# The opening of a conformer block's first FFN, loaded and scheduled in another order

## The chip, the cores and the metric

One kernel launch runs on one core of a Trainium2 chip. The metric is the device time of that launch in microseconds (us). TensorE (PE) multiplies, VectorE (DVE) and ScalarE (ACT) do the elementwise work, GpSimd (POOL) a few small operations, and SyncE (SP) issues the transfers from the chip's memory. Each engine takes its own instructions in the order in which the built program lists them; engines wait for each other through semaphores.

## The reference, cut to what matters

The block works on 256 tokens with 2048 channels, all in float32:

```
ada = silu(c) @ w_ada + b_ada                      # 9 vectors of 2048: shift, scale, gate, three times
h = rms_norm(x, ffn1_norm) * (1 + sc1) + sh1
x = x + 0.5 * g1 * (silu(h @ Wg) * (h @ Wu)) @ Wdown    # FFN 1, 5632 wide
h = rms_norm(x, mix_norm) * (1 + scm) + shm
x = x + gm * mixer(h)                              # differential attention and a causal convolution
h = rms_norm(x, ffn2_norm) * (1 + sc2) + sh2
x = x + 0.5 * g2 * (silu(h @ Wg2) * (h @ Wu2)) @ Wdown2 # FFN 2
```

The change concerns FFN 1, and within it mostly the stretch before and just after the first product with a weight. What must be there before that product: silu(c), the first 128 scale and the first 128 shift values of the modulation (each a dot product of c with a row of `w_ada`), the sums of squares of all 256 tokens, and the first weight tile.

## The kernel before, in words

Every weight is read once, as a tile of 128 x 2048 floats (1 MB): four row tiles of 128 input channels by 512 output columns. A product with a weight is made of three passes (L232, L233, L234): both operands are split into a rounded high part and the exact remainder, and the kernel adds high x high, high x low, low x high. So each weight row tile goes through ACT, which rounds it (`whi`, L222), and through DVE, which subtracts (`wlo`, L224). A row tile takes six passes, three for each of two token tiles. Weights land in four buffers (`raw`), which the adaLN rows share: 144 tiles of `w_ada` (L151) are each multiplied with c and summed in one DVE instruction (L152), two of them (a scale and a shift) for each 128 channels.

FFN 1 is cut into 22 chunks of 256 gate and 256 up columns (here c0 to c21). Stage A takes the first row tiles of every chunk, into two accumulators, which ACT then copies out (L345, one copy for each token tile, t0 and t1). How many row tiles a chunk takes in stage A is in `EXT`: the modulation comes one 128-channel tile at a time, so the first chunks take fewer. After stage A `n_a2` chunks get the rest of their first piece and the second piece, the last `n_a3` of them also the third; then all chunks are finished in turn, and the down projection follows.

The code is written in the order of the work, and a scheduler that has its own idea of durations places the instructions on each engine. Its order is fixed when the program is built. `issue_after` holds an instruction back behind another, and `AHEAD` makes weight loads go three chunks ahead of their products.

At the start (L101 to L112) c comes in as a row, is spread over the 128 partitions by four products with a row of ones (L110) and goes through Silu. The tokens come in by column pieces of 512 (L569), both token tiles in each; squares are summed on ACT for token tile 0 and on DVE for token tile 1 (L255, L252). `Norm.begin` (L272) scales and transposes the tokens of one token tile, and `Norm.tile` (L288) modulates and splits one 128-channel tile: DVE scales and shifts, ACT rounds, DVE subtracts, one after the other. `Norm.tile` is also used, with `fine`, at the two later places where the residual stream changes: from FFN 1 to the mixer, and from the mixer to FFN 2.

## Time and profile before

| | |
|---|---|
| times of three runs | 1870.46, 1874.54, 1874.64 us |
| their median | 1874.54 us |
| the profiled execution: span from first to last instruction (the page gives no other time for it) | 1872.4 us |
| PE busy | 1838.1 us (98%) |
| DVE busy | 1439.3 us (77%) |
| ACT busy | 905.5 us (48%) |
| moved by the transfers | 495.92 MB, 265 GB/s on average |
| first pass with a weight starts | 21.79 us |
| granted TensorE clock, mean | 0.995 |

In rows of the timeline the first column is the start in us from the start of the span, the second how long the group of instructions lasts, then engine, source line and operation, what it writes and reads, the shape, and how many; in brackets how long the engine had been idle before and what ended the idle time. Rows of the stretches give, for each stretch, its length, each engine's busy time with the number of its instructions, the granted clock of PE, the share of the transfer engines in use, and GB/s. Rows of groups give the number of instructions, then their busy time and the mean of one in ns. A PE pass of 512 columns is recorded with the time until its result is out, so passes overlap; what one costs is the distance between two starts.

### The profile page before, as it was taken

Reading aid. Unit: us, or ns where it says so; the run is one execution under the profiler, and the core shown is the slowest. Engines: PE = TensorE matmul, PEld = TensorE weight load, DVE = VectorE, ACT = ScalarE, POOL = GpSimd, SP = SyncE. Lnnn points to the kernel's source line nnn. Section 1 sums busy time; section 2 is a strip of 40 time slices with the busy share of each in tenths; the row PEclk is TensorE's granted clock in tenths of the full one; section 3 lists DMA queues with packets and bytes.
Section 4 is the critical chain, followed back from the end, with each engine's and each line's share of the span. In section 5 each row is a group of like instructions: output and inputs, shape, how many; then the busy total and the mean of one; then the engine's idle time right before and its main releaser. Section 6 shows DMA issues by size and latency. Waiting matters only on the chain.

```text
span 1872.4 us, 21954 instructions
## 1 busy us (share of the span) xinstructions
PE 1838.1 (98%) x8295; PEld 1510.8 (81%) x8295; DVE 1439.3 (77%) x1921; ACT 905.5 (48%) x1363; POOL 30.9 (2%) x34
## 2 busy tenths in 40 slices
PE   6999999999999999999999999999999999999999
PEld 3788888888888888778877788888888888888887
DVE  6779889988888777789999688775877755544443
ACT  4654354444444434454876555654444444433332
POOL 0000000000000000000110100000000000000000
PEclk9999999999999999999999899999999999999999
DMA  8888978888898888646343696895777755555552
GB/s 312 341 315 328 364 272 327 330 326 329 317 345 330 335 340 333 226 170 210 137 158 138 241 344 257 328 355 202 274 285 272 275 197 180 190 215 205 201 212 79
DMA packets 72141, 495.92 MB, mean 265 GB/s; under 512 B 8114, under 2 KB 8290, under 8 KB 14052
## 3 DMA queue, kind: packets, MB, share of 16 engines
q1 hardware_dynamic: 72036, 494.53, 71.5%
q8 instruction: 65, 1.06, 0.2%
q14 instruction: 40, 0.33, 0.1%
HBM read 492.37 MB, written 2.12 MB: 264 GB/s over the span
## 4 chain that ended last, share of the span: by engine, by line
PE 91%; DVE 5%; ACT 2%; issue 1%; DMA 1%; POOL 1%; POOLq 0%; ACTq 0%; DVEq 0%
PE acc L233 29%; PE acc L234 29%; PE acc L232 29%; DVE wlo L224 1%; DVE blk L596 1%; PE tp L426 1%; DMA raw<-in_w_ada_dram 1%; PE acc L677 1%; DVE raw L152 1%; PE tp L285 0%; ACT whi L222 0%; PE acc L110 0%; PE tp L740 0%; POOL rs L129 0%; ACT tmp L632 0%
## 5 line engine op out<-in xcount | busy, mean ns | idle before, releaser
L222 ACT CAST whi<-raw 128x1024 fp32r<-128x1024 f32 (+1 forms) x624 | 645.7, 1042 | 773.1 <-PE acc L234 665.9
L224 DVE TENSOR_TENSOR wlo<-raw,whi 128x1024 fp32r<-128x1024 f32 (+1 forms) x624 | 747.5, 1210 | 349.6 <-ACT whi L222 348.6
L232 PE MATMUL acc<-whi,blk 128*128 128x512 f32 x2464 | 966.2, 394 | 12.2 <-ACT whi L222 6.2
L233 PE MATMUL acc<-wlo,blk 128*128 128x512 f32 x2464 | 965.1, 392 | 3.5 <-DVE wlo L224 3.5
L234 PE MATMUL acc<-whi,blk 128*128 128x512 f32 x2464 | 964.8, 392 | 0.5 <-DVE blk L319 0.5
L232 PEld LDWEIGHTS acc<-whi,blk 128*128 128x128 f32 x2464 | 464.2, 189 | 110.0 <-ACT whi L222 8.3
L233 PEld LDWEIGHTS acc<-wlo,blk 128*128 128x128 f32 x2464 | 464.9, 189 | 101.6 <-DVE wlo L224 6.7
L234 PEld LDWEIGHTS acc<-whi,blk 128*128 128x128 f32 x2464 | 464.8, 189 | 97.3 <-DVE blk L319 0.9
L152 DVE CUSTOM_DVE_ANT_0 raw<-raw,c_bc 128x2048 f32<-128x2048 f32 x144 | 328.9, 2285 | 5.2 <-DMA raw<-in_w_ada_dram 5.2
L596 DVE SCALAR_TENSOR_TENSOR blk<-blk,cst,blk 128x256 f32<-128x256 f32 x240 | 100.9, 483 | 0.0
L345 ACT COPY blk<-acc 128x512 f32<-128x512 f32 x88 | 51.0, 589 | 84.6 <-PE acc L234 81.3
L422 DVE TENSOR_TENSOR blk<-acc,blk 128x512 f32<-128x512 f32 x88 | 56.8, 684 | 0.5 <-PE acc L234 0.5
L233 PE MATMUL acc<-blk,blk 128*128 128x512 f32 x96 | 37.4, 391 | 0.5 <-DVE blk L224 0.5
L232 PE MATMUL acc<-blk,blk 128*128 128x512 f32 x96 | 37.8, 394 | 0.0
L234 PE MATMUL acc<-blk,blk 128*128 128x512 f32 x96 | 37.4, 390 | 0.0
L424 DVE TENSOR_TENSOR blk<-blk 128x256 f32<-128x256 f32 x88 | 34.7, 420 | 0.8 <-ACT blk L423 0.7
L423 ACT ACTIVATE blk<-blk 128x256 f32<-128x256 f32 x88 | 33.3, 409 | 2.6 <-DVE blk L422 1.7
L244 DVE TENSOR_TENSOR blk<-tp,blk 128x512 fp32r<-128x512 f32 x44 | 30.0, 685 | 0.9 <-ACT blk L243 0.8
L224 DVE TENSOR_TENSOR blk<-raw,blk 128x1024 fp32r<-128x1024 f32 x24 | 28.7, 1221 | 0.8 <-ACT blk L222 0.8
L426 PEld LDWEIGHTS tp<-cst,blk 128*128 128x128 f32 x176 | 21.6, 140 | 5.6 <-DVE blk L244 0.3
L243 ACT CAST blk<-tp 128x512 fp32r<-128x512 f32 x44 | 25.3, 581 | 1.6 <-PE tp L426 1.6
L426 PE MATMUL tp<-cst,blk 128*128 128x128 f32 x176 | 26.0, 272 | 0.0
(134 smaller groups left out, 624.1 us busy)
## 6 DMA issues: line engine op xcount, KB each, us to landing
raw<-in_w_gu_dram SPq DMA_DIRECT2D x165, 1024.0 KB, 4.9
raw<-in_w_ada_dram SPq DMA_DIRECT2D x144, 1024.0 KB, 5.7
raw<-in_w_dn_dram SPq DMA_DIRECT2D x88, 1024.0 KB, 4.8
raw<-in_w_in_dram SPq DMA_DIRECT2D x40, 1024.0 KB, 4.8
raw<-in_w_out_dram SPq DMA_DIRECT2D x16, 1024.0 KB, 5.4
raw<-in_w_gu_dram SPq DMA_DIRECT2D x8, 768.0 KB, 7.0
raw<-in_w_gu_dram SPq DMA_DIRECT2D x6, 512.0 KB, 6.6
blk<-gate_line SPq DMA_DIRECT2D x6, 512.0 KB, 6.6
```

The lines of the kernel that those rows point to most:

```text
L152: nc.vector.tensor_tensor_reduce(out=raw, in0=raw, in1=c_bc, scale=1.0, scalar=0.0, op0=ALU.mult, op1=ALU.add, accum_out=ada_cols[g][:, j ...
L222: nc.scalar.copy(out=hi[:, :m, :], in_=raw[:, h:h + m, :])
L224: nc.vector.tensor_sub(out=lo[:, :m, :], in0=raw[:, h:h + m, :], in1=hi[:, :m, :].bitcast(F32))
L232: nc.tensor.matmul(acc, ah, wh, start=start, stop=False)
L233: nc.tensor.matmul(acc, ah, wl, start=False, stop=False)
L234: nc.tensor.matmul(acc, al, wh, start=False, stop=stop)
L345: last_part[0] = nc.scalar.copy(out=parts[c][:, t, :], in_=accs[t])
L422: nc.vector.tensor_add(out=p[:, t, :], in0=accs[t], in1=p[:, t, :])
L423: nc.scalar.activation(out=p[:, t, :256], in_=p[:, t, :256], func=AF.Silu)
L424: nc.vector.tensor_mul(out=p[:, t, 256:], in0=p[:, t, :256], in1=p[:, t, 256:])
L426: nc.tensor.transpose(tp[:, i, t * P:(t + 1) * P], p[:, t, 256 + i * P:256 + (i + 1) * P], ident)
L596: nc.vector.scalar_tensor_tensor(out=y, in0=u, scalar=w, in1=y, op0=ALU.mult, op1=ALU.add)
```

## The change

What it does:

- The packed small parameters go first on the transfer queue and carry c as 16 columns; c is put through Silu there (128 x 16) and spread by 16 transposes and four ACT copies.
- The tokens come in by token tile (two transfers of 1 MB) into a tile of their own, `xall`. The pool `blk` has 28 buffers instead of 32, since the tokens no longer lie in it. The squares of each token tile are shared by ACT and DVE.
- The first scale row and shift row of `w_ada` come in halves, four transfers of 512 KB into `blk` buffers, and are reduced in four DVE instructions (`first_modulation`).
- The first chunks' weights (one row tile each) also land in `blk` buffers (`w_first`), c3 and c4 in one transfer, c5 and c6 in another.
- Six float32 products of the identity with pieces of token tile 1 are put on PE ahead of the first products with weights; nothing reads them.
- `Norm.tile` rounds on ACT straight from the transposed tokens while DVE scales and shifts the same values; then DVE subtracts. In the opening both token tiles go through it at once (256 columns).
- `EXT` goes from 3 chunks with one row tile, 3 with two, 5 with three to 7, 4 and 3; `FIRST_ADA` says after which loads an adaLN row is issued. FFN 1 now takes 11 chunks with 3 of them further (`n_a2`, `n_a3`) where it took 8 with 2.

```diff
-AHEAD = 3       # weight tiles that go ahead of the first products
-EXT = (1,) * 3 + (2,) * 3 + (3,) * 5   # row tiles of the first chunks in stage A
+WARM = 6
+AHEAD = 3
+EXT = (1,) * 7 + (2,) * 4 + (3,) * 3
+LOADS = [(0,), (1,), (2,), (3, 4), (5, 6)] + [(c,) for c in range(7, NCH)]
+FIRST_ADA = (0, 0, 1, 1, 1, 1, 1, 0, 1, 1, 1, 1)
...
+    nc.sync.dma_start(out=cst[:, :first_cols], in_=small[:, :first_cols])
+    for t in range(NT):
+        nc.sync.dma_start(out=xall[:, t, :], in_=x_in[t * P:(t + 1) * P, :])
...
+    nc.scalar.activation(out=c_col, in_=col("c"), func=AF.Silu)
+    c_bc = const.tile([P, D], F32, name="c_bc")
+    for i in range(4):
+        pc = acc_tile()
+        for j in range(4):
+            k = 4 * i + j
+            nc.tensor.transpose(pc[:, j * P:(j + 1) * P], c_col[:, k:k + 1].to_broadcast([P, P]), ident)
+        nc.scalar.copy(out=c_bc[:, i * 512:(i + 1) * 512], in_=pc)
...
+    def first_modulation():
...
+        for i in range(2):
+            for h in range(2):
+                wa = blk([P, 1024])
+                hs = slice(1024 * h, 1024 * h + 1024)
+                nc.sync.dma_start(out=wa, in_=w_ada[i, :, hs])
+                nc.vector.tensor_tensor_reduce(out=wa, in0=wa, in1=c_bc[:, hs], scale=1.0, scalar=0.0, op0=ALU.mult,
+                                               op1=ALU.add, accum_out=a[:, 2 * i + h:2 * i + h + 1])
...
+    def w_first(cs):
...
+        raw = blk([P, 2, 512])
+        w_dma[0] = nc.sync.dma_start(out=raw[:, :n, :], in_=w_gu1[cs[0]:cs[0] + n, 0].rearrange("c p n -> p c n")[:, :, :512])
+        hi = whp.tile([P, 2, 512], F32R, tag="whi", name=nm("whi"))
+        lo = wlp.tile([P, 2, 512], F32R, tag="wlo", name=nm("wlo"))
+        nc.scalar.copy(out=hi[:, :n, :], in_=raw[:, :n, :])
+        nc.vector.tensor_sub(out=lo[:, :n, :], in0=raw[:, :n, :], in1=hi[:, :n, :].bitcast(F32))
...
-            nc.vector.tensor_scalar(out=hf[:, j, :], in0=tp[:, j, :], scalar1=G, scalar2=SH, op0=ALU.mult,
-                                    op1=ALU.add)
-            nc.scalar.copy(out=hi, in_=hf[:, j, :])
-            self.last = nc.vector.tensor_sub(out=self.hl[kb][:, j, t * P:(t + 1) * P], in0=hf[:, j, :],
-                                             in1=hi.bitcast(F32))
+            nc.scalar.activation(out=hi, in_=src, func=AF.Identity, scale=G, bias=SH)
+            nc.vector.tensor_scalar(out=hf, in0=src, scalar1=G, scalar2=SH, op0=ALU.mult, op1=ALU.add)
+            self.last = nc.vector.tensor_sub(out=self.hl[k // 4][:, k % 4, ts], in0=hf, in1=hi.bitcast(F32))
...
+            for i in range(WARM):
+                nc.tensor.matmul(acc_tile(), ident, x[i % 4][:, 1, :], start=True, stop=True)
+            first_modulation()
+            begin_ready()
+            for i in range(len(LOADS) + AHEAD):
+                if i < len(LOADS):
+                    load(i)
+                    with tc.issue_after(w_dma[0].ins):
+                        if i < len(FIRST_ADA):
+                            ada_until(ada_next[0] + FIRST_ADA[i])
+                        else:
+                            ada_share(ada_a[0], ada_a[1])
+                        begin_ready()
+                if i >= AHEAD:
+                    cs = LOADS[i - AHEAD]
...
+                    for c in cs:
+                        stage_a(c, ws[c], [acc_tile() for _ in range(NT)], (0, 1), ext[c])
...
-    ffn(norm1, w_gu1, w_dn1, 32, (0.78, 32), (0.74, 100), norm_m, 8, 2)
+    ffn(norm1, w_gu1, w_dn1, 32, (0.78, 32), (0.74, 100), norm_m, 11, 3)
```

How this moves instructions is told at three places. The first is the opening on PE and on DVE. On PE before, four products spread c, two groups of transposes turn the tokens, and the weights follow:

```order
L110 MATMUL acc_100<-blk_86,tmp_87 128x512
L285 MATMUL tp_149<-cst,tmp_147 128x128 x4
L285 MATMUL tp_161<-cst,tmp_159 128x128 x4
L232 MATMUL acc_220<-whi_184,blk_145 128x512
L233 MATMUL acc_220<-wlo_186,blk_145 128x512
```

On PE now (L130 spreads c, L424 are the unread products, L344 turns the tokens, L270 is the first pass with a weight):

```order
L130 MATMUL acc_115<-cst,c_col 128x128 x4
L424 MATMUL acc_168<-xall,cst 128x512
L424 MATMUL acc_170<-xall,cst 128x512
L344 MATMUL tp_146<-cst,tmp_152 128x128 x2
L344 MATMUL tp_147<-cst,tmp_152 128x128 x2
L424 MATMUL acc_172<-xall,cst 128x512
L424 MATMUL acc_174<-xall,cst 128x512
L344 MATMUL tp_146<-cst,tmp_162 128x128 x2
L344 MATMUL tp_147<-cst,tmp_162 128x128 x2
L424 MATMUL acc_176<-xall,cst 128x512
L424 MATMUL acc_178<-xall,cst 128x512
L270 MATMUL acc_237<-whi_203,blk_144 128x512
```

The unread products stand between the transposes, not in one block. On DVE now, from the end of token tile 1's squares (L206 reduces half an adaLN row, L304 and L135 belong to token tile 1's norm, L342 scales its tokens):

```order
L304 TENSOR_REDUCE rstd_158<-ss_125 128x1
L206 ISA blk_182,adah_181<-blk_182,c_bc 128x1024
L206 ISA adah_181 128x1
L135 TENSOR_SCALAR rstd_158<-rstd_158 128x1
L342 TENSOR_SCALAR tmp_162<-xall,rstd_158 128x512
L206 ISA blk_185,adah_181<-blk_185,c_bc 128x1024
```

The first half row stands ahead of the norm's second step, and the other halves behind the scaling of the tokens.

The second place is ACT in stage A. Before, from the copies of c5 on (acc_350 and acc_351 are c5's accumulators, acc_381 and acc_382 those of c6; whi_281 and whi_285 are c6's weights, whi_311 and whi_315 those of c7, whi_338 of c8):

```order
L345 COPY blk_364<-acc_350 128x512
L345 COPY blk_364<-acc_351 128x512
L222 CAST whi_281<-raw_279 128x1024
L295 CAST blk_145<-tmp_154 128x128
L295 CAST blk_145<-tmp_166 128x128
L222 CAST whi_285<-raw_279 128x512
L345 COPY blk_401<-acc_381 128x512
L222 CAST whi_311<-raw_309 128x1024
L222 CAST whi_315<-raw_309 128x512
L345 COPY blk_401<-acc_382 128x512
L222 CAST whi_338<-raw_336 128x1024
L222 CAST whi_342<-raw_336 128x512
```

On ACT now, from the copies of c6 on (acc_342 and acc_343 belong to c6, acc_368 and acc_369 to c7, acc_399 and acc_400 to c8; whi_270 is c7's weight, whi_296 c8's, whi_327 c9's, whi_355 c10's):

```order
L392 COPY blk_350<-acc_342 128x512
L392 COPY blk_350<-acc_343 128x512
L249 CAST whi_270<-raw_268 128x1024
L392 COPY blk_382<-acc_368 128x512
L392 COPY blk_382<-acc_369 128x512
L249 CAST whi_296<-raw_294 128x1024
L330 ACTIVATE blk_144<-tp_147,ada_180,scales 128x256
L392 COPY blk_413<-acc_399 128x512
L249 CAST whi_327<-raw_325 128x1024
L392 COPY blk_413<-acc_400 128x512
L249 CAST whi_355<-raw_353 128x1024
```

The weights of c7 are rounded behind both copies of c6, those of c8 behind both copies of c7, those of c9 behind the first copy of c8, those of c10 one chunk ahead. Further on, c5 and c6 (one cast) stand behind the first copy of c4, c11 behind the first copy of c10, c12 behind the first copy of c11, and c13 one chunk ahead.

The third place is ACT around c14 now (acc_524 and acc_525 are c12, acc_560 and acc_561 c13, acc_597 c14; whi_479 and whi_483 are c14's weights, whi_512 and whi_516 those of c15, whi_549 of c16):

```order
L392 COPY blk_544<-acc_524 128x512
L392 COPY blk_544<-acc_525 128x512
L318 ACTIVATE tmp_770<-xall,rstd_158 128x512
L392 COPY blk_580<-acc_560 128x512
L392 COPY blk_580<-acc_561 128x512
L249 CAST whi_479<-raw_477 128x1024
L249 CAST whi_483<-raw_477 128x1024
L249 CAST whi_512<-raw_510 128x1024
L249 CAST whi_516<-raw_510 128x1024
L392 COPY blk_623<-acc_597 128x512
L392 COPY blk_623<-acc_598 128x512
L249 CAST whi_549<-raw_547 128x1024
```

The weights of c14 stand behind both copies of c13; from c15 on every cast is one chunk ahead of its products, as it was before from c8 on.

More of the change, by code (lines that the diff above doesn't have):

```diff
@@ L65, in block_kernel @@
 @with_exitstack
-def block_kernel(ctx: ExitStack, tc: tile.TileContext, x_in, c_in, pos_in, w_ada, small, w_gu1, w_dn1,
+def block_kernel(ctx: ExitStack, tc: tile.TileContext, x_in, pos_in, w_ada, small, w_gu1, w_dn1,
                  w_in, w_out, w_gu2, w_dn2, out):
@@ L99, in tp_tile @@
         return tpp.tile(list(shape), F32, tag="tp", name=nm("tp"))
-    c_bc = const.tile([P, D], F32, name="c_bc")
-    c_row = [blk([1, 1024]) for _ in range(2)]
-    ones_r = tmp([1, P])
-    nc.gpsimd.memset(ones_r, 1.0)
-    for i in range(2):
-        nc.sync.dma_start(out=c_row[i], in_=c_in[:, i * 1024:(i + 1) * 1024])
-        for j in range(2):
-            pc = acc_tile()
-            nc.tensor.matmul(pc, ones_r, c_row[i][:, j * 512:(j + 1) * 512], start=True, stop=True)
-            o = (2 * i + j) * 512
-            nc.scalar.activation(out=c_bc[:, o:o + 512], in_=pc, func=AF.Silu)
     cst = const.tile([P, NCOLS], F32, name="cst")
     pos_i = const.tile([P, NT], I32, name="pos_i")
+    xall = const.tile([P, NT, D], F32, name="xall")
+    x = [xall[:, :, n * 512:(n + 1) * 512] for n in range(4)]
+    first_cols = _COLS["nm"][0]
+    nc.sync.dma_start(out=cst[:, :first_cols], in_=small[:, :first_cols])
+    for t in range(NT):
+        nc.sync.dma_start(out=xall[:, t, :], in_=x_in[t * P:(t + 1) * P, :])
     def col(name):
@@ L120, in block_kernel @@
     ident = col("ident")
+    c_col = const.tile([P, KT], F32, name="c_col")
     identb = const.tile([P, P], BF16, name="identb")
@@ L147, in ada @@
         g = j // 8
-        if j % 8 == 0:
+        if g not in ada_cols:
             ada_cols[g] = const.tile([P, 8], F32, name=f"ada{g}")
@@ L156, in ada @@
             nc.vector.tensor_add(out=ada_cols[g][:, o:o + 2], in0=ada_cols[g][:, o:o + 2], in1=cst[:, p0:p0 + 2])
-    ada_next = [0]
+    ada_next = [2]
     credit = [0.0]
@@ L353, in pieces @@
                             st.piece(kb, t)
[L355 removed]
         ext = [4] * NCH
         if not st.done:
[L359 to L376 removed]
+            raws, begun = st.begin_both(), [0]
@@ new lines, in ffn, with load, begin_ready @@
+            ws = {}
+            def load(i):
+                cs = LOADS[i]
+                if ext[cs[0]] == 1:
+                    ws.update(zip(cs, w_first(cs)))
+                else:
+                    ws[cs[0]] = w_tile(w_gu[cs[0], 0], False, (0, ext[cs[0]]))
+            for c in range(NCH):
+                ext[c] = EXT[c] if c < len(EXT) else 4
+            def begin_ready():
+                while begun[0] < 4 and base + 2 * begun[0] + 2 <= ada_next[0]:
+                    st.tile(raws[begun[0]], tmp([P, S]), (begun[0], slice(0, S)))
+                    begun[0] += 1
@@ L566, in block_kernel @@
     norm2 = Norm(96, "n2", sm([P, NT, 4], "ss"))
-    for n in range(4):
-        b = blk([P, NT, 512])
-        nc.sync.dma_start(out=b, in_=x_in[:, n * 512:(n + 1) * 512].rearrange("(t p) n -> p t n", p=P))
-        x.append(b)
-        for t in range(NT):
-            square_sum(n, t, norm1.ss, t == 1)
-    first_cols = _COLS["nm"][0]
-    nc.sync.dma_start(out=cst[:, :first_cols], in_=small[:, :first_cols])
-    ffn(norm1, w_gu1, w_dn1, 32, (0.78, 32), (0.74, 100), norm_m, 8, 2)
+    for t in range(NT):
+        for n in range(4):
+            square_sum(n, t, norm1.ss, n % 2 == 1)
+    ffn(norm1, w_gu1, w_dn1, 32, (0.78, 32), (0.74, 100), norm_m, 11, 3)
     st = norm_m
```

65 lines of the change are left out of this document (35 added, 30 removed).

## The prediction

> **What bounds the kernel now.** I read the page first, then the stretches, then PE's rows in the stretch that the change touches.
>
> ```profile
> span 1872.4 us, 21954 instructions
> PE 1838.1 (98%) x8295; PEld 1510.8 (81%) x8295; DVE 1439.3 (77%) x1921; ACT 905.5 (48%) x1363; POOL 30.9 (2%) x34
> ...
> 20.00:60.00 40.00, 30.88 (x108) 22.88 (x109) 30.58 (x48) 21.28 (x38) 0.00 (x0) 0.91 0.90 331
> 60.00:100.00 40.00, 40.00 (x182) 32.94 (x181) 32.04 (x39) 24.64 (x35) 0.00 (x0) 1.00 0.95 365
> 180.00:260.00 80.00, 80.00 (x358) 66.17 (x357) 65.58 (x76) 35.17 (x43) 0.00 (x0) 1.00 0.87 327
> ```
>
> PE is the bound: 34.3 us of the span are not PE time, and from 60 us on its stretches are full. The number of passes does not change, so only the time lost before PE becomes dense counts. These rows show that loss:
>
> ```profile
> 21.79 0.79 PE L232 MATMUL acc<-whi,blk 128*128 128x512 f32 x1 [5.61 <-ACT blk L295]
> ...
> 27.34 0.39 PE L234 MATMUL acc<-whi,blk 128*128 128x512 f32 x1
> 29.35 0.73 PE L232 MATMUL acc<-whi,blk 128*128 128x512 f32 x2 [1.62 <-ACT whi L222]
> 30.89 0.73 PE L232 MATMUL acc<-whi,blk 128*128 128x512 f32 x2 [0.81 <-ACT whi L222]
> ...
> 38.99 0.40 PE L234 MATMUL acc<-whi,blk 128*128 128x512 f32 x1
> 41.80 0.84 PE L232 MATMUL acc<-whi,blk 128*128 128x512 f32 x2 [2.41 <-ACT whi L222]
> 43.53 0.79 PE L233 MATMUL acc<-wlo,blk 128*128 128x512 f32 x1 [0.89 <-DVE wlo L224]
> ...
> 49.66 0.39 PE L234 MATMUL acc<-whi,blk 128*128 128x512 f32 x1
> 50.97 0.73 PE L232 MATMUL acc<-whi,blk 128*128 128x512 f32 x2 [0.92 <-ACT whi L222]
> 52.23 0.50 PE L233 MATMUL acc<-wlo,blk 128*128 128x512 f32 x1 [0.52 <-DVE wlo L224]
> ...
> 54.18 0.39 PE L233 MATMUL acc<-wlo,blk 128*128 128x512 f32 x1
> ...
> 59.85 0.39 PE L234 MATMUL acc<-whi,blk 128*128 128x512 f32 x1
> ```
>
> 25 passes lie between the last two rows: 5.67 / 25 = 0.227 us each. The last stall ends at 52.23. By then c0 to c6 are done (3 x 6 + 3 x 12 + 18 = 72 passes) and two of c7. A stall-free stream that is at 74 passes at 52.23 would have begun at 52.23 - 74 x 0.227 = 35.4. I call this the **virtual start**; what the change wins in FFN 1 is how far it moves it.
>
> The waits at 29.35, 41.80 and 50.97 have one cause: ACT rounds the next weights only behind a copy of accumulators, which waits for PE.
>
> ```profile
> 49.38 0.59 ACT L345 COPY blk<-acc 128x512 f32<-128x512 f32 x1 [6.19 <-PE acc L234]
> 49.87 1.57 ACT L222 CAST whi<-raw 128x1024 fp32r<-128x1024 f32 x2
> ```
>
> Here c7's cast had 6.19 us of idle ACT before it, and starts only behind c6's first copy.
>
> **The change: the opening.** Durations, and the rate at which data comes in:
>
> ```profile
> L152 DVE CUSTOM_DVE_ANT_0 raw<-raw,c_bc 128x2048 f32<-128x2048 f32 x4 | 9.1, 2290 | 1.7 <-DMA raw<-in_w_ada_dram 1.7
> L110 PE MATMUL acc<-blk,tmp 1*128 1x512 f32 x8 | 7.2, 1072 | 2.3 <-DMA blk<-in_c_dram 2.3
> L252 DVE CUSTOM_DVE_ANT_0 tmp<-blk 128x512 f32<-128x512 f32 x4 | 2.8, 692 | 8.6 <-DMA blk<-in_x_dram 6.3 <-PE acc L110 2.0 <-ACT tmp L255 0.4
> L255 ACT ACTIVATE tmp<-blk 128x512 f32<-128x512 f32 x4 | 2.5, 618 | 0.0
> L222 ACT CAST whi<-raw 128x512 fp32r<-128x512 f32 x3 | 1.9, 618 | 5.7 <-DMA raw<-in_w_gu_dram 5.6
> L285 PE MATMUL tp<-cst,tmp 128*128 128x128 f32 x8 | 2.0, 424 | 4.7 <-DVE tmp L280 4.7
> L282 ACT ACTIVATE tmp<-blk,rstd 128x512 f32<-128x512 f32 x1 | 0.7, 716 | 0.0
> L129 POOL TENSOR_TENSOR rstd<-rstd,half 128x1 f32<-128x1 f32 x2 | 1.1, 570 | 12.1 <-DVE rstd L128 12.1
> L280 DVE TENSOR_SCALAR tmp<-blk,rstd 128x512 f32<-128x512 f32 x2 | 1.0, 486 | 0.7 <-POOL rstd L129 0.7
> L295 ACT CAST blk<-tmp 128x128 fp32r<-128x128 f32 x3 | 0.9, 298 | 1.0 <-DVE tmp L293 1.0
> ...
> 3.00:4.50 1.50, 1.50 (x3) 0.66 (x2) 0.00 (x0) 0.11 (x1) 0.00 (x0) 1.00 1.00 248
> 4.50:6.00 1.50, 1.50 (x3) 0.47 (x2) 0.54 (x1) 0.49 (x1) 0.00 (x0) 1.00 1.05 391
> 6.00:9.00 3.00, 3.00 (x5) 0.86 (x3) 0.86 (x4) 1.19 (x2) 0.00 (x0) 1.00 0.91 306
> 9.00:12.00 3.00, 0.47 (x1) 0.00 (x0) 1.54 (x5) 2.49 (x8) 0.00 (x0) 1.00 1.06 432
> ```
>
> Parameters and tokens are 2.25 MB. At the shown rates they are in at 9.7, at 432 GB/s from 4.5 us on at 8.7; I take 9.2 for token tile 1. ACT's two squares with their read-out end at 10.7, the sum at 10.9. The first half row stands ahead of the norm's second step: a half lies between 692 and 2290 ns by length, 1.15 us to the next. So 12.05, the norm step 0.15, POOL 0.57 with some 0.3 of waiting, the scaling 0.49: 13.5. Three halves and four small sums (3 x 1.15 + 0.75) give 17.7. The rounding of 256 columns is bounded by 298 (128) and 716 ns (512): 0.45, half of it and of the waits hidden by nothing, 18.2; then c0's cast, which stands behind it, 0.62: **18.85**, with bounds 18.0 and 19.8. Before it was 21.79. The low part costs another 0.42 of waiting. The transfers are not late here: at 432 GB/s a half row takes 1.2 us and c0's weights 0.6, so these are in at 9.2 + 4 x 1.2 + 0.6 = 14.6, over 3 us ahead of their cast.
>
> The sixteen transposes for c cost 16 x 0.25 = 4 us where four products took 7.2; both are done before the tokens are summed and hide behind their transfer; without that cover they would cost those 4 us.
>
> The **six unread products** read token tile 1, so they start at 9.2. L110 is their nearest row: two records of 1.07 each make 1.79 us a product, half of that with the clock up. All six with eight transposes take 12.7 us if the clock never rises (PE free at 21.9, 3 us late) and about 8 if it rises on the way (17.2). The stretches show when it rises:
>
> ```profile
> 42.00:43.00 1.00, 0.64 (x2) 0.09 (x1) 1.00 (x3) 0.93 (x3) 0.00 (x0) 0.63 1.00 354
> 43.00:44.00 1.00, 0.47 (x1) 0.47 (x2) 1.00 (x4) 0.19 (x1) 0.00 (x0) 0.50 0.96 326
> 48.00:49.00 1.00, 1.00 (x4) 0.80 (x3) 0.00 (x0) 0.00 (x0) 0.00 (x0) 0.50 1.02 332
> 49.00:50.00 1.00, 1.00 (x5) 0.52 (x3) 0.00 (x0) 0.62 (x2) 0.00 (x0) 0.96 0.95 330
> ```
>
> It fell at about 42.26 and was back at 49.08, 6.8 us later, with dense work only from 43.53. So I take it up at 16 us at the latest, PE free at 17 to 19, and the products cost nothing.
>
> **The change: what follows.** The order in which ACT stands now is fixed, and the rows above price each place. A cast behind both copies of the chunk before: its first pass came 29.35 - 27.34 = 2.01 after the last pass, the low part 52.23 - 50.97 = 1.26 later, 3.27 in all, where a dense stream needs 3 x 0.227: **2.59 lost**. A cast behind the first copy only: 52.23 - 49.66 - 0.68 = **1.89 lost**. One chunk ahead: none.
>
> - c7, c8, c14 stand behind both copies: 7.77.
> - c9, c11, c12 behind the first: 5.67. c5 with c6 too, with four high passes to run meanwhile: 2.57 - 5 x 0.227 = 1.44.
> - c13's cast is ahead, but an adaLN reduction of 2.3 us and its sums stand on DVE between c12's and c13's low parts: about 0.75.
>
> With 0.42 that is 16.05, and the virtual start 18.85 + 16.05 = 34.9: **0.5 us earlier**, for an opening that is 2.9 us earlier. Twelve row tiles leave stage A (56 in place of 68); theirs are the same passes, later. Three more chunks with two additions each on DVE (three pairs like the next row, 4.1 us) hide in the 14 us that DVE has free in 180 to 260; uncovered they would cost 4.
>
> ```profile
> 174.17 1.38 DVE blk L412 x2
> ...
> 769.35 0.50 PE L232 MATMUL acc<-whi,blk 128*128 128x512 f32 x1 [0.36 <-ACT blk L295]
> ```
>
> `Norm.tile` at the two later places can win at most the wait for its rounding, which the second row has at the end of FFN 1; I take 0.3. A reading of the transposes by two engines at once is unpriced here, bounded by one more rounding, 0.3 of loss.
>
> Sum against the profiled execution: 1872.4 - 0.5 - 0.3 = 1871.6; the median of the runs lies 2.1 above that span, so 1873.7 with the clock up throughout. Now the clock. Half of the 6.8 us it was down is 3.41. In the 3.41 us ahead of its fall (from 38.85) PE had passes until 39.2 and two from 41.80, some 0.8 us; in 28.6 to 32.0 it waited 1.62 and 0.81 us, had some 1.5 us of passes, and the clock stayed up. A loss of 2.59 leaves 0.8 to 0.9 us of passes in its worst 3.4 us. With three of them and the gap ahead of c0, one fall is likelier than none. One costs 13 passes at twice the time, 2.6 us, as at 43.53 to 49.08. **Forecast: 1876.3.**
>
> [...]
>
> **Rivals.** *No fall of the clock*: PE's waits stay under the 2.41 that preceded the one fall; against it stand three stalls in place of one. 1873.7. *The lead carries through*: if casts did not wait for copies, DVE would be the limit. From c2's low part, at 20.7, to c14's it has nine reductions of 2.25 (20.3), fourteen subtractions of weights (at the row below for whole pairs, half for single row tiles: 14.3) and 4.2 of modulation: 59.5. PE would be at 168 passes (c0 to c14) at 63.2, virtual start 25.1, 1863.6. ACT's row with 6.19 us of idle time ahead of a cast speaks against it.
>
> ```profile
> L224 DVE TENSOR_TENSOR wlo<-raw,whi 128x1024 fp32r<-128x1024 f32 (+1 forms) x624 | 747.5, 1210 | 349.6 <-ACT whi L222 348.6
> ```
>
> *Slower: the clock falls at c7 or c8 and stays down.* [...] Ten passes in each of c7, c8 and c9 and six of c10 at 0.2 us more: 7.2, so 1880.9, and 1883.5 with a second fall at c14. [...] *The unread products don't raise the clock*: c0 to c2 lose 15 x 0.2 = 3.0, 1876.7, or PE is free only at 21.9, as much again.
>
> **Chances.** A measurement of this kernel tells 0.3% (5.6 us) from no change: faster is below 1868.9, slower above 1880.2. One fall or a cold beginning (1874.5 to 1879) 0.40; no fall (1871 to 1874.5) 0.23; clock down for long 0.25; lead carried 0.08; something unpriced 0.04, on the fast side. So faster 0.12, same 0.63, slower 0.25. The range leaves out the lead and the second fall: 1869 to 1882.5.
>
> **What would show it.** Right: first weight pass near 18.9 with six products done by 19; ACT copies with PE waits just ahead of the casts of c7, c8 and c14; PE waits for `whi` of 1.6 to 1.8 us there; dense PE only from about 68 us; granted clock under 1 once between 30 and 75. Wrong: casts of c7 to c9 that run while the chunk before is on PE, or dense work from 50 us on; PE waits for the transfers of `w_gu`; new waits between 100 and 260 us, where the adaLN rows of the second piece come.

## The result, and the profile after

The changed kernel takes 1879.66 us (median of 5 runs, 1879.22 to 1881.57); the kernel before takes 1874.54 (5 runs, 1870.46 to 1875.89). The ratio is 1.0032, with a 95% interval of 1.0021 to 1.0044: slower by about 5 us, which lies on the 0.3% that counts as a difference here. The forecast was 1876.3 with a range of 1869 to 1882.5.

The profiled execution of the changed kernel (1879.22 us) has a span of 1877.4, 5.0 longer than before's. Its span, and its stretches (columns as before: PE busy, loads, DVE, ACT, POOL, granted clock, transfers):

```profile
span 1877.4 us, 21980 instructions
...
20.00:60.00 40.00, 31.14 (x113) 22.00 (x112) 29.37 (x37) 23.13 (x38) 0.00 (x0) 0.91 0.84 307
60.00:100.00 40.00, 37.30 (x163) 29.75 (x162) 32.65 (x37) 23.40 (x33) 0.00 (x0) 1.00 0.94 344
100.00:760.00 660.00, 660.00 (x2961) 545.88 (x2960) 556.45 (x678) 297.97 (x355) 0.00 (x0) 1.00 0.86 321
1160.00:1320.00 160.00, 159.05 (x711) 131.02 (x710) 125.39 (x143) 90.67 (x122) 0.00 (x0) 1.00 0.86 323
```

Two places have idle PE that before did not have: 60 to 100 us, which was full, and 1160 to 1320, which was full too. PE's rows in the opening and in stage A:

```profile
15.02 1.88 PE L424 MATMUL acc<-xall,cst 128*128 128x512 f32 x4
18.59 0.51 PE L270 MATMUL acc<-whi,blk 128*128 128x512 f32 x1 [1.69 <-ACT whi L263]
19.72 0.50 PE L271 MATMUL acc<-wlo,blk 128*128 128x512 f32 x1 [0.63 <-DVE wlo L264]
...
32.22 0.39 PE L272 MATMUL acc<-whi,blk 128*128 128x512 f32 x1
34.31 0.73 PE L270 MATMUL acc<-whi,blk 128*128 128x512 f32 x2 [1.70 <-ACT whi L249]
35.57 0.50 PE L271 MATMUL acc<-wlo,blk 128*128 128x512 f32 x1 [0.53 <-DVE wlo L251]
...
39.78 0.73 PE L270 MATMUL acc<-whi,blk 128*128 128x512 f32 x2 [1.62 <-ACT whi L249]
41.03 0.79 PE L271 MATMUL acc<-wlo,blk 128*128 128x512 f32 x1 [0.53 <-DVE wlo L251]
...
71.30 0.74 PE L270 MATMUL acc<-whi,blk 128*128 128x512 f32 x2 [1.18 <-ACT whi L249]
72.56 0.51 PE L271 MATMUL acc<-wlo,blk 128*128 128x512 f32 x1 [0.52 <-DVE wlo L251]
```

The unread products end at 16.9, the first pass with a weight starts at 18.59, and then c7 (34.31), c8 (39.78) and, further on, c9, c11, c12 and c14 wait for their rounded weights. The last stall ends at 72.56, with 146 passes ahead of that point, so the virtual start is 72.56 - 146 x 0.2267 = 39.5, against 35.4 (35.45 without rounding). ACT shows why:

```profile
33.18 1.08 ACT L249 CAST whi<-raw 128x1024 fp32r<-128x1024 f32 x1
37.50 1.28 ACT L392 COPY blk<-acc 128x512 f32<-128x512 f32 x2 [3.24 <-PE acc L272]
38.68 1.05 ACT L249 CAST whi<-raw 128x1024 fp32r<-128x1024 f32 x1
```

The cast at 38.68 (c8's) stands behind two copies, and these waited 3.24 us for PE to finish c7. PE then waits 1.62 us for the cast.

To see where the rest of the 5.0 us is, I follow three waits that both programs have: the one for a low part at the mixer's first taps (DVE's steps of the convolution), the one for a weight at the mixer's end, and the start of the last pass. In before:

```profile
833.39 0.50 PE L233 MATMUL acc<-wlo,blk 128*128 128x512 f32 x1 [1.10 <-DVE wlo L224]
...
1072.32 0.51 PE L232 MATMUL acc<-whi,blk 128*128 128x512 f32 x1 [0.44 <-ACT whi L222]
...
1867.47 0.39 PE L234 MATMUL acc<-blk,blk 128*128 128x512 f32 x1
```

In the changed kernel, with the two waits of FFN 2 that before does not have:

```profile
835.91 0.50 PE L271 MATMUL acc<-wlo,blk 128*128 128x512 f32 x1 [1.10 <-DVE wlo L251]
...
1074.88 0.50 PE L270 MATMUL acc<-whi,blk 128*128 128x512 f32 x1 [0.42 <-ACT whi L249]
...
1156.54 0.50 PE L271 MATMUL acc<-wlo,blk 128*128 128x512 f32 x1 [0.71 <-DVE wlo L251]
...
1241.01 0.50 PE L271 MATMUL acc<-wlo,blk 128*128 128x512 f32 x1 [0.95 <-DVE wlo L251]
...
1872.38 0.39 PE L272 MATMUL acc<-blk,blk 128*128 128x512 f32 x1
```

Four stretches come out of these starts, in us (the other kernels are those of the experiments below, read at the same waits):

| kernel | virtual start | to the mixer's taps | mixer | FFN 2 to the last pass |
|---|---|---|---|---|
| before | 35.45 | 797.94 | 238.93 | 795.15 |
| changed | 39.46 | 796.45 | 238.97 | 797.50 |
| changed, casts first | 31.26 | 796.61 | 241.03 | 797.52 |
| changed, eight products | 39.25 | 796.45 | 241.34 | 797.48 |
| before, casts first | 30.49 | 799.83 | 240.79 | 795.15 |
| before, 0.70 rows | 34.47 | 797.43 | 239.36 | 796.36 |
| before, tile function and 0.70 rows | 33.65 | 798.20 | 241.26 | 797.44 |

So stage A costs the change 4.0, of which 1.5 come back before the mixer's taps, and FFN 2 costs 2.35. Of the 1.5, 0.7 are no gain: two groups of four transposes (0.36 us each) lie ahead of the last stall in the changed kernel, and behind it in before, and the virtual start counts passes only. Stage A proper lost 3.3. All these stretches come from one profiled execution of each kernel.

### The profile page after: what moved, and what is told of

It is laid out like the page before. It is cut to its first block, busy times and chain, and to the rows that moved or that the text cites. A ratio compares the mean times of both kernels' runs of the same rounds, so it can differ in the third digit from the quotient of the medians.

```text
span 1877.4 us, 21980 instructions
## 1 busy us (share of the span) xinstructions
PE 1841.4 (98%) x8315; PEld 1511.0 (80%) x8315; DVE 1442.9 (77%) x1924; ACT 909.6 (48%) x1360; POOL 30.8 (2%) x33
## 4 chain that ended last, share of the span: by engine, by line
PE 90%; DVE 5%; ACT 2%; issue 1%; POOL 0%; DMA 0%; SPq 0%; POOLq 0%; ACTq 0%; DVEq 0%
PE acc L271 29%; PE acc L272 29%; PE acc L270 29%; DVE wlo L251 2%; DVE blk L655 1%; PE tp L490 1%; ACT whi L249 1%; PE acc L736 1%; DMA blk<-in_w_ada_dram 0%; DVE raw L159 0%; PE tp L321 0%; PE tp L799 0%; ACT blk L392 0%; POOL rs L136 0%; DVE blk L206 0%
## 5 line engine op out<-in xcount | busy, mean ns | idle before, releaser
L270 PE MATMUL acc<-whi,blk 128*128 128x512 f32 x2464 | 964.8, 394 | 10.1 <-ACT whi L249 7.3
L270 PEld LDWEIGHTS acc<-whi,blk 128*128 128x128 f32 x2464 | 463.2, 188 | 108.4 <-ACT whi L249 9.9
L159 DVE CUSTOM_DVE_ANT_0 raw<-raw,c_bc 128x2048 f32<-128x2048 f32 x142 | 324.3, 2285 | 14.1 <-DMA raw<-in_w_ada_dram 13.9
L270 PE MATMUL acc<-blk,blk 128*128 128x512 f32 x96 | 37.4, 391 | 0.0
L487 ACT ACTIVATE blk<-blk 128x256 f32<-128x256 f32 x88 | 33.7, 412 | 6.9 <-DVE blk L486 5.9
L361 DVE TENSOR_SCALAR tmp<-tp,scales,ada 128x128 f32<-128x128 f32 x48 | 17.2, 404 | 11.8 <-PE tp L321 11.5
```

What stands on the lines that cost most here:

```text
L159: nc.vector.tensor_tensor_reduce(out=raw, in0=raw, in1=c_bc, scale=1.0, scalar=0.0, op0=ALU.mult, op1=ALU.add, accum_out=ada_cols[g][:, j ...
L270: nc.tensor.matmul(acc, ah, wh, start=start, stop=False)
L487: nc.scalar.activation(out=p[:, t, :256], in_=p[:, t, :256], func=AF.Silu)
```

## The experiments

**ACT's order in stage A.** The changed kernel, with each copy of an accumulator held behind the cast of the next load; the same work is done.

```diff
-                last_part[0] = nc.scalar.copy(out=parts[c][:, t, :], in_=accs[t])
+                with tc.issue_after(behind.ins) if behind else nullcontext():
+                    last_part[0] = nc.scalar.copy(out=parts[c][:, t, :], in_=accs[t])
...
-                        stage_a(c, ws[c], [acc_tile() for _ in range(NT)], (0, 1), ext[c])
+                        stage_a(c, ws[c], [acc_tile() for _ in range(NT)], (0, 1), ext[c], casts.get(i - AHEAD + 1))
```

> The changed kernel, with one thing different: in stage A of FFN 1 each copy of an accumulator on ACT stands behind the cast of the next load's weights, so that ACT rounds one load ahead throughout. Theory (ACT's order eats the lead): PE's waits for whi at c7, c8, c9, c11, c12 and c14 (1.70, 1.62, 0.93, 0.94, 0.50, 1.18 us in the changed kernel, with 0.5 for the low part behind each) go, dense PE begins well before 60 us, the virtual start moves from 39.5 to 25 to 29, and the time falls by 10 to 14 us against the changed kernel, to 1866 to 1869. Rival (DVE or the transfers bound this place anyway): the waits for whi turn into waits for wlo or for transfers of the same size, and the time stays within 2 us of 1879.7.

1870.84 us (11 runs), ratio to before 0.9982 (0.9973 to 0.9991). That is 0.5% less than the changed kernel's 1.0032, some 9 us: the theory's cause holds, but the gain lies below its 10 to 14. The version is also 0.2% under before, clear of its interval, though less than the 0.3% that counts as a difference here. The largest and the last of PE's waits in stage A that are left:

```profile
40.38 0.73 PE L271 MATMUL acc<-whi,blk 128*128 128x512 f32 x2 [1.79 <-ACT whi L250]
...
64.36 0.50 PE L272 MATMUL acc<-wlo,blk 128*128 128x512 f32 x1 [0.53 <-DVE wlo L252]
```

ACT ahead of the first of them (a cast, then copies):

```profile
39.29 1.04 ACT L250 CAST whi<-raw 128x1024 fp32r<-128x1024 f32 x1 [3.40 <-DMA raw<-in_w_gu_dram]
40.24 1.06 ACT L394 COPY blk<-acc 128x512 f32<-128x512 f32 x2
```

Virtual start 64.36 - 146 x 0.2267 = 31.3, 8.2 earlier. Not all of that is ACT's order: 1.9 are there before c2, because in this profile the clock came up later (at 15.1), the unread products lasted until 18.25, and the clock did not fall at c0; it fell once, at 42.4. The changed kernel with 0.78 adaLN rows (below) has the same stage A as the changed kernel, and its clock also falls once between the first pass and 80 us (at 69.24); there the 181st pass with a weight starts at 78.59, here at 72.24. With one fall in each, the order is worth 6.35. The cast at 39.29 now stands ahead of the copies of the chunk before, and waits 3.40 us for its transfer, not for PE: with ACT out of the way the transfer of the weights is next, and the virtual start stops at 31.3, outside the 25 to 29 that was expected.

**The six products left out** (`WARM = 6` to `WARM = 0`; nothing of the output depends on them).

> The changed kernel without the six unread products (nothing of the output depends on them). In the changed kernel the clock was up from 13.85 to 20.31 us and fell then all the same. Theory (the products are worth next to nothing, since the clock falls again at 20.3 and c1 to c4 run into it): first weight pass at 18.3 to 18.6, the clock up from 22 to 24 us on, time within 1.6 us of the changed kernel's, 1878 to 1881. Rival 1 (they keep the opening warm): c0 to c4 run at half clock for longer, 15 to 25 passes at 0.2 us more, 3 to 5 us slower, 1882.5 to 1885. Rival 2 (they cost: PE or the banks of the accumulators are busy when the first passes want them): 2 to 4 us faster, 1876 to 1878.

1881.43 us (5 runs), ratio 1.0041 (1.0028 to 1.0054), 1.8 above the changed kernel with intervals that overlap. The virtual start is 72.61 - 33.10 = 39.5, that of the changed kernel: what the products win at the beginning is gone by c14. The theory's reason is borne out, its 1881 was 0.4 too low, and the loss of 3 to 5 did not come.

**The opening with the old row plan**, on the changed kernel:

```diff
-EXT = (1,) * 7 + (2,) * 4 + (3,) * 3
-LOADS = [(0,), (1,), (2,), (3, 4), (5, 6)] + [(c,) for c in range(7, NCH)]
-FIRST_ADA = (0, 0, 1, 1, 1, 1, 1, 0, 1, 1, 1, 1)
+EXT = (1,) * 3 + (2,) * 3 + (3,) * 5
+LOADS = [(c,) for c in range(NCH)]
+FIRST_ADA = (0, 0, 2, 0, 1, 1, 1, 0, 1, 1, 0, 1)
...
-    ffn(norm1, w_gu1, w_dn1, 32, (0.78, 32), (0.74, 100), norm_m, 11, 3)
+    ffn(norm1, w_gu1, w_dn1, 32, (0.78, 32), (0.74, 100), norm_m, 8, 2)
```

> The changed kernel's opening (tokens by tile, adaLN pair in halves, transposes for c, unread products, the new tile function) with the row tiles of before: 3 chunks of one, 3 of two, 5 of three, each chunk its own load, the adaLN plan and the two numbers of the second stage of before. Theory (the opening is a gain, the 7, 4, 3 rows with their casts behind copies lose it): first weight pass near 18.6, stalls like those of before (1.6, 0.8, 2.4, 0.9 us for whi) about 3 us earlier, the virtual start at 32 to 33.5 where before has 35.4, and 1871 to 1873. Rival (the row tiles are not it: adaLN columns or transfers of the opening are late in either plan): dense PE begins no earlier than before, 1875 to 1879.

1877.83 us (9 runs), ratio 1.0023 (1.0014 to 1.0033): neither answer. The time lies in the rival's range, but not for its reason: PE is dense earlier than in before, even earlier than the theory said, and the gain is lost later. PE's rows, from the last stall of stage A on:

```profile
38.98 0.73 PE L270 MATMUL acc<-whi,blk 128*128 128x512 f32 x2 [1.62 <-ACT whi L249]
...
46.35 0.50 PE L271 MATMUL acc<-wlo,blk 128*128 128x512 f32 x1 [0.53 <-DVE wlo L251]
...
765.74 0.63 PE L321 MATMUL tp<-cst,tmp 128*128 128x128 f32 x4 [2.17 <-DVE tmp L316]
766.91 0.50 PE L270 MATMUL acc<-whi,blk 128*128 128x512 f32 x1 [0.55 <-ACT blk L330]
...
833.63 0.80 PE L271 MATMUL acc<-wlo,blk 128*128 128x512 f32 x1 [2.65 <-DVE wlo L251]
```

The last stall ends at 46.35 with 74 passes: a virtual start of 29.6, 5.9 before that of before. All of it is gone at the mixer's taps (833.63, before 833.39). A wait of 1.01 at 170.67 takes the first 1.1. At the end of FFN 1 PE waits 2.17 and 0.55 us for the mixer's first activations, the clock falls right behind that (from 768.76 on the passes start 0.43 us apart in place of 0.23), and at the taps PE waits 2.65 where before has 1.10. DVE there, in this kernel and then in before:

```profile
829.59 2.85 DVE L655 SCALAR_TENSOR_TENSOR blk<-blk,cst,blk 128x256 f32<-128x256 f32 x7
832.36 2.35 DVE L251 TENSOR_TENSOR wlo<-raw,whi 128x1024 fp32r<-128x1024 f32 x2
```

```profile
827.54 1.22 DVE L224 TENSOR_TENSOR wlo<-raw,whi 128x1024 fp32r<-128x1024 f32 x1
...
830.53 1.67 DVE L596 SCALAR_TENSOR_TENSOR blk<-blk,cst,blk 128x256 f32<-128x256 f32 x4
832.11 2.35 DVE L224 TENSOR_TENSOR wlo<-raw,whi 128x1024 fp32r<-128x1024 f32 x2
```

The order differs: before subtracts one part of the weights (827.54) ahead of these taps. The row plan of stage A, with the two counts of the stage behind it, has changed the order 780 us later. The plan also decides how many adaLN columns are there when the mixer begins (99 here, 96 in the changed kernel, 100 in before), but that this is what turned the order was not tested.

**The tile function alone**, on the kernel before:

```diff
+            nc.scalar.activation(out=hi, in_=tp[:, j, :], func=AF.Identity, scale=G, bias=SH)
...
-            nc.scalar.copy(out=hi, in_=hf[:, j, :])
```

> The kernel before, with one thing different: in the tile function ACT rounds out of the accumulator bank itself, beside DVE's modulation, as the change has it, where before it rounds what DVE wrote. Theory: it saves part of the 0.3 to 0.4 us wait at the ends of FFN 1 and the mixer, 0 to 0.6 us in all, no measurable difference: 1874 to 1875. Rival (two engines on one bank delay each other, and this is the 1 us by which the changed kernel's span grew beyond FFN 1): 1 to 1.5 us slower than before, 1875.5 to 1876.

1873.76 us (11 runs), ratio 1.0002 (0.9994 to 1.0011): no difference, as the theory had it.

**Casts first, on the kernel before** (the same edit of the copies).

> The kernel before, with one thing different: as in the run on the changed kernel, each copy of an accumulator in stage A of FFN 1 stands on ACT behind the cast of the next load's weights. Theory (ACT's order is the limit of stage A in either kernel): the waits for whi of before (1.62 and 0.81 us at c3 and c4, 2.41 at c6, 0.92 at c7) go, and with them the fall of the clock at 42 us; virtual start 28 to 31 in place of 35.4, 1867.5 to 1870.5, level with the changed kernel in the same order (1870.8), so that the new opening itself adds little. Rival 1 (the order costs only where rows go 7, 4, 3): within 1.5 us of before. Rival 2 (an early end of FFN 1 is given back where the mixer begins, as with the old row plan on the new opening, where PE waited 2.17 us there for DVE): the virtual start moves as in the theory, and the time stays at 1873 or above.

1872.07 us (11 runs), ratio 0.9990 (0.9982 to 0.9999). The virtual start moves to 47.27 - 74 x 0.2267 = 30.5, as the theory has it (the fall of the clock at 42, priced at 2.6 us in the prediction, is gone with the waits), but only 1.9 us of the 5.0 arrive, and 1.2 in the profiled execution. There 1.9 go to two waits of PE in FFN 1, of which before has only the first, with 0.40, and 1.9 to the mixer (240.79), whose length also changes with the clock, as the last section shows:

```profile
173.10 0.50 PE L234 MATMUL acc<-wlo,blk 128*128 128x512 f32 x1 [0.97 <-DVE wlo L225]
...
322.41 0.69 PE L430 MATMUL tp<-cst,blk 128*128 128x128 f32 x4 [0.96 <-DVE blk L428]
```

So ACT's order limits stage A in either kernel, and Rival 2 is right that the lead is given back, though at other places than it named. With casts first the two openings start within 0.8 us of each other (31.3 and 30.5): the new opening's early start is no longer seen.

**Eight unread products in place of six** (`WARM = 8`).

> The changed kernel with eight unread products in place of six (nothing of the output depends on them). In its profile the six end at 16.9, PE waits 1.69 us for c0's weights, and the clock is down from 20.31 to 23.72, while c0 to c4 run. Theory (the gap ahead of c0 makes that fall): the products end at 18.5 to 19, the clock stays up to c7, 15 passes at the full clock in place of half, 1.7 us: 1877.5 to 1878.5. Rival 1 (the clock is still down where the products begin, so that eight end at 20 or later): first weight pass 0.5 to 1.5 us later, 1879.5 to 1881. Rival 2 (the fall has another cause): clock down near 20 all the same, 1879 to 1880.

1881.34 us (5 runs), ratio 1.0037 (1.0023 to 1.0051), no better than six, and above all three answers. PE's rows:

```profile
15.61 3.60 PE L424 MATMUL acc<-xall,cst 128*128 128x512 f32 x8
18.86 0.58 PE L270 MATMUL acc<-whi,blk 128*128 128x512 f32 x1
...
27.89 1.19 PE L270 MATMUL acc<-whi,blk 128*128 128x512 f32 x4 [1.01 <-ACT whi L263]
...
32.96 0.73 PE L270 MATMUL acc<-whi,blk 128*128 128x512 f32 x2 [1.71 <-ACT whi L249]
34.22 0.79 PE L271 MATMUL acc<-wlo,blk 128*128 128x512 f32 x1 [0.53 <-DVE wlo L251]
```

The gap ahead of c0 is closed, the granted clock is 1.00 from 13.2 to 33.7 us, and c5 starts at 27.89 where the changed kernel has 29.23. So the theory's cause of that fall holds. Two profiles with six products bear it out: with casts first and with 0.78 adaLN rows on the changed kernel the clock came up only at 15.1 and 14.6, the products lasted until 18.25 and 17.90, left no gap or one of 0.22 ahead of c0, and the clock did not fall there. But the clock then falls at c7 (to 0.50 at 33.7; the pass at 34.22 takes 0.79), where six products left it up (1.00 from 23.79 to 40.85), and again at c8 (at 40.5): the virtual start is 39.25, 0.2 better.

**More adaLN rows in FFN 1's second stage.** The rate goes from 0.74 to 0.80 a weight tile, on the changed kernel, and with casts first:

```diff
-    ffn(norm1, w_gu1, w_dn1, 32, (0.78, 32), (0.74, 100), norm_m, 11, 3)
+    ffn(norm1, w_gu1, w_dn1, 32, (0.78, 32), (0.80, 100), norm_m, 11, 3)
```

> The changed kernel, with one thing different: the second stage of FFN 1 asks for 0.80 adaLN rows with a weight tile in place of 0.74 (the limit of 100 columns stays). In the changed kernel some 97 columns are there at 760 us where before has 100, and 8 to 10 instructions of reductions more lie between 1160 and 1320 us, where PE waits 0.71 and 0.95 us for low parts that stand behind them on DVE; before has neither wait. Theory (those rows are the part of the loss that lies beyond stage A): both waits go, 1.2 to 2 us faster than the changed kernel, 1877.6 to 1878.5. Rival (the rows only collide elsewhere): new waits of PE for wlo between 100 and 840 us, or at the mixer's beginning, and 1879 to 1882.

> The changed kernel with both: copies behind the next cast in stage A, and 0.80 adaLN rows with a weight tile in the second stage of FFN 1. Theory: the two gains add, as they lie 1100 us apart: 1.2 to 2 us below the run with the casts first alone (1870.8), 1868.8 to 1869.6, 4 to 5 below before. Rival: with PE 8 us earlier DVE is the limit of the second stage's beginning, and the rows added there make waits for wlo of the same size: 1870 to 1872.

1882.07 us (5 runs, 1.0051, 1.0037 to 1.0064) and 1877.07 (11 runs, 1.0022, 1.0013 to 1.0032): 2.4 and 6.2 worse than without (the intervals overlap for the first pair, not for the second). The waits of FFN 2 at 1156 and 1241 are gone in both (another, of 0.86, stands at 1149 and at 1140); but PE now waits in FFN 1 (0.78 at 592, 0.19 at 598, 0.79 at 654 us in the first) and 2.67 us at the mixer's taps, in the order of the old row plan. That is the rival's reason; the second run is 5 us beyond its range.

With 0.78, all 100 columns are there and the taps stand as in before. Casts first with 0.78, and the changed kernel with 0.78:

> The changed kernel with the copies of stage A behind the next cast, and 0.78 adaLN rows with a weight tile in the second stage of FFN 1 (0.74 in the change, 0.80 in the earlier runs). With 0.78 all 100 columns of the limit are there when the mixer begins, as in before (96 in the changed kernel), and DVE's subtractions of weights at the mixer's first taps stand as in before (with 0.80 one stood behind seven more taps, and PE waited 2.66 us there). Theory (FFN 2's loss is the four late columns): the stretch from the mixer's end to the last pass takes 795 to 796.5 us in place of 797.7, and the time is 1.2 to 2.4 below the casts first alone (1870.8): 1868.5 to 1869.7. Rival (the earlier rows collide in FFN 1 again, as with 0.80, where three waits of 1.8 us in all stood at 584 to 646 us): 1870.5 to 1873.

> The changed kernel with one thing different: 0.78 adaLN rows with a weight tile in the second stage of FFN 1. Theory (the four late columns cost FFN 2 its 2.35 us): 1.2 to 2.4 faster than the changed kernel, 1877.3 to 1878.5. Rival (they collide in FFN 1 instead, as with 0.80): 1879.3 to 1881.

1875.04 us (11 runs, 1.0004, 0.9995 to 1.0013) and 1881.83 (5 runs, 1.0047, 1.0033 to 1.0060): slower than the rivals said, and not for their reason, since the waits of FFN 1 are not there. In FFN 2 the theory comes true: counted from the same pass as in the table (the 3440th from the end), it takes 795.8 us in both, 1.7 less than with 96 columns, and as much as with the tile function alone on the kernel before (below). But the time is lost elsewhere. What is new in the first of the two is at the end of FFN 1, and by the taps (830.50) it is 2.6 behind casts first alone (827.87); the mixer takes 2.3 more, with the clock down for 17.1 us in place of 13.7:

```profile
764.81 0.63 PE L322 MATMUL tp<-cst,tmp 128*128 128x128 f32 x4 [1.72 <-DVE tmp L317]
765.99 0.50 PE L271 MATMUL acc<-whi,blk 128*128 128x512 f32 x1 [0.55 <-ACT blk L331]
```

**What makes FFN 2 longer.** The other way round: the kernel before with fewer rows (0.74 to 0.70), so that its mixer begins with 96 columns as in the changed kernel; then the same with the tile function.

> The kernel before, with one thing different: 0.70 adaLN rows with a weight tile in the second stage of FFN 1 in place of 0.74, so that the mixer begins with 96 columns, as in the changed kernel, in place of 100. Nothing of the opening or of FFN 1's row tiles is touched, and the same work is done. Theory (the four late columns are what FFN 2 loses in the changed kernel): PE waits of 0.6 to 1.0 us for low parts near 1154 and 1238 us, 797.3 to 798 us from the mixer's end (the wait for whi near 1072) to the last pass in place of 795.4, and 1.5 to 2.4 us slower than before, 1875.3 to 1876.5. Rival (FFN 2's loss comes from another part of the change, such as 28 buffers in place of 32): no such waits, 795 to 796 us, 1873.3 to 1874.5.

> The kernel before with two things different: the change's tile function (ACT rounds out of the bank beside DVE) and 0.70 adaLN rows with a weight tile in the second stage of FFN 1, so that the mixer begins with 96 columns, as in the changed kernel. Either alone left FFN 2 nearly as it was: 796.0 and 796.4 us from the wait for whi at the mixer's end to the last pass, where before has 795.4 and the changed kernel 797.7. DVE's order in FFN 2 is now that of the changed kernel, but for two subtractions that stand ahead of a piece's low parts instead of behind. Theory (the two together make FFN 2's loss: three reductions in a row behind four modulations): the wait of 0.7 us near 1154 us appears, and 796.7 to 797.8 us from the mixer's end to the last pass. Rival (the loss depends on where the transfers of FFN 2's weights are, which the opening sets): no wait above 0.4 us near 1154, and 795.4 to 796.5. In time, with what 96 columns save in FFN 1 (1.5 us at 832 us in the run with 0.70): 1874.5 to 1876 by the theory, 1873 to 1874.5 by the rival.

0.70 alone: 1875.91 us (11 runs), ratio 1.0005 (0.9996 to 1.0013), FFN 2 at 796.36, 1.2 longer, with no wait near 1154 (but one of 0.53 at 1257.90): between theory and rival. With the tile function: 1876.99 us (11 runs), ratio 1.0014 (1.0005 to 1.0023), FFN 2 at 797.44, and the wait is there, as the theory has it; the time is 1.0 above its range (these figures run from start to start; the expectations of these two runs counted the last pass's 0.23 in for before and the changed kernel). DVE in the last:

```profile
1146.74 2.28 DVE L152 CUSTOM_DVE_ANT_0 raw<-raw,c_bc 128x2048 f32<-128x2048 f32 x1
...
1148.95 2.29 DVE L152 CUSTOM_DVE_ANT_0 raw<-raw,c_bc 128x2048 f32<-128x2048 f32 x1
...
1151.16 2.29 DVE L152 CUSTOM_DVE_ANT_0 raw<-raw,c_bc 128x2048 f32<-128x2048 f32 x1
...
1153.45 2.35 DVE L224 TENSOR_TENSOR wlo<-raw,whi 128x1024 fp32r<-128x1024 f32 x2
```

And PE:

```profile
1154.72 0.50 PE L233 MATMUL acc<-wlo,blk 128*128 128x512 f32 x1 [0.72 <-DVE wlo L224]
```

Three reductions of late columns stand in a row, behind the modulations of the new tile function (the last one's subtraction ends at 1146.8), and the low part comes behind them. The wait is 0.72 where the changed kernel has 0.71, with before's opening and row plan. So these two together make 2.3 of the 2.35 us: the tile function alone costs FFN 2 0.7 us (795.82), the late columns alone 1.2, both 2.3. Neither alone moves the time by more than its interval.

## Why the prediction was right, and where not

Predicted was +1.8 us against before: 0.5 earlier with the clock up, 0.3 from the tile function, and 2.6 for one fall of the clock. The profiled execution has +5.0. Point by point:

- **First weight pass at 18.85:** 18.59. The products were done at 16.9 and cost nothing, as forecast. *"The low part costs another 0.42 of waiting"* was too little: the second pass came at 19.72, 1.13 behind the first where a stream needs 0.23, 0.9 lost.
- **ACT's order:** right, and the largest term. A cast behind both copies was priced at 2.59; c7 lost (34.31 - 32.22 - 0.23) + (35.57 - 34.31 - 0.45) = 2.67, c8 by the same sum 2.59, c14 2.24, as four transposes filled part of its gap. One copy was priced at 1.89; c9 and c11 lost 1.90, c12 1.55, with transposes too. c5 with c6 lost 1.51 (1.44 forecast), c13 0.63 (0.75). All eight: 15.0 against 15.6. That the order is the cause is shown by the run with casts first: the virtual start moved by 8.2, by 6.35 with one fall of the clock in each.
- **The virtual start at 34.9 with the clock up:** with two falls of 1.6 taken off, 39.5 - 3.2 = 36.2. The profile with 0.78 adaLN rows agrees: its clock stays up from before the first pass until the end of the last stall (69.13), and its virtual start is 36.0. The 1.3 too much are the low part (0.5), the 0.7 of transposes that the sum left out, and about 1.0 of slower passes behind each stall (the pass after the one at 35.57 comes 0.33 later, not 0.23), less 0.3 of the first pass and 0.6 of the stalls.
- **One fall of the clock, 2.6 us:** mis-sized. It fell twice, to 0.50 at 20.37, behind the wait ahead of c0, and at 40.85, at c8; the clock under 1 once between 30 and 75 us was forecast rightly, the first one not. Each fall lasted 3.4 us and cost 1.6 (9 passes in 3.64 us from 20.29 on, 8 in 3.43 from 41.03 on, at 0.227 each): together 3.2. That half of the 6.8 us in before is the stretch to look at was an estimate; here the clock's changes lie whole multiples of 3.41 us apart (last section). The rival in which the clock stays down was nearer in time (1880.9), but by luck: its 36 slower passes, up to the sixth of c10, were an estimate, and the clock came back at 23.79 and 44.27.
- **`Norm.tile` wins 0.3 and three more chunks hide:** between stage A and the taps the changed kernel needs 0.8 less after the transposes are taken out, and it has no wait from 100 to 760 us. But the step *"Twelve row tiles leave stage A (56 in place of 68); theirs are the same passes, later"* failed: it counted passes, and did not ask how many adaLN columns are there when the mixer begins (96, before 100). With the tile function, whose loss was bounded at 0.3, these late columns make FFN 2 2.35 longer, for which the sum held no term.

One reading of before was wrong, though no price rests on it: of the three waits to which the prediction gives one cause, the one at 41.80 has another. Its cast began only when the transfer of the weights had landed:

```profile
40.70 1.04 ACT L222 CAST whi<-raw 128x1024 fp32r<-128x1024 f32 x1 [0.69 <-DMA raw<-in_w_gu_dram]
```

With casts first on the kernel before, a wait of 1.04 is left at that place (40.58).

The four stretches give 3.3 (stage A) - 0.8 (to the taps) + 0.0 (the mixer) + 2.35 (FFN 2) = 4.9 of the 5.0. The time was inside the range, and that is luck in part: the upper end made room for a clock that is down for long, which did not come, and the room was used by a second short fall and by FFN 2's term. The forecast itself was 3.4 us low, more by FFN 2's term than by any other. The lead did not carry through (25.1 was that rival's virtual start, which by the sum's own terms gives 1863.9, not 1863.6): even with casts first it is 31.3, as a transfer is late next. That the products don't raise the clock is refuted by the passes at 15.02, four records in 1.88 us where the first four took 2.62, with a granted clock of 0.50 from 10.13 to 13.55 us and of 1.00 from there to 20.37; their gain was lost at c0's wait.

What makes the changed kernel better is one edit away: with casts first it takes 1870.84, 2.9 us below the kernel before as measured beside it. Its virtual start would give 4.2; in its profiled execution (1873.24, the longest of the 11) the mixer takes back 2.1 and FFN 2 2.4, with 1.3 won ahead of the taps. A plan of columns that avoids FFN 2's loss without a new one elsewhere was not found with rates of 0.78 and 0.80.

## What to carry to other kernels

On an engine that runs in order, a copy that drains an accumulator must not stand ahead of the work that the next product needs: price each such place by its row (here 1.9 to 2.7 us), and a start that is 3 us earlier is gone after two of them. An opening that is won early is only won if what comes due later keeps its place, so count how much of the background work (here the adaLN columns) is done at each change of stage, before and after, and follow two or three waits that both programs share through to the end. Losses under the interval of a comparison still add up: the tile function and the late columns, neither of which showed in the time alone, made FFN 2 2.3 us longer together.
